# Ten half-size landing tiles for the weights in place of five, and what was moved along with them, in a two-layer hybrid decoder kernel

## The chip, the cores and the metric

The kernel runs on one core of one Trainium2 chip. The metric is the device time of one launch in microseconds (us). Three runs of the kernel before gave 985.4, 985.72 and 986.92 us, a median of 985.72 us. Five engines work side by side and wait for each other by semaphores: TensorE (PE, with its weight load PEld), VectorE (DVE), ScalarE (ACT), GpSimd (POOL) and SyncE (SP). SP computes nothing here: it issues transfers, one after the other, and a transfer that has to wait holds all that stand behind it in SP's list. ACT and POOL issue a few transfers too.

## The reference

Two layers, each with an FFN, a mixer of three attention groups, and a second FFN, over 256 tokens of width 1024, all in float32:

```python
for l in range(DEPTH):                                     # DEPTH = 2
    h = h + 0.5 * swiglu(rms_norm(h, ffn1_norm[l]), ffn1_w_gate[l], ffn1_w_up[l], ffn1_w_down[l])
    h = h + hybrid_mixer(rms_norm(h, mix_norm[l]), w_in[l], ..., w_out[l], cos, sin)
    h = h + 0.5 * swiglu(rms_norm(h, ffn2_norm[l]), ffn2_w_gate[l], ffn2_w_up[l], ffn2_w_down[l])
# swiglu(x, g, u, d) = (silu(x @ g) * (x @ u)) @ d,  the inner width is 2816
```

The mixer projects to 3592 columns, runs a top-64 sparse attention (A, four heads), a block attention (B, four heads) and a forgetting attention with a gate (C, eight heads), and projects back to 1024. All weights, some 190 MB, are read from HBM once.

## The kernel before

**Weights as a stream.** Every product of float32 numbers is made of three matmuls: a number is split into a rounded high part and the rest, and high by high, high by low and low by high are summed in PSUM. So each piece of weights goes through three hands: a transfer brings it into a landing tile (`raw`), ACT makes the high part (`wh`, L278), DVE subtracts to get the low part (`wl`, L282), and PE uses both. The piece in which ACT, DVE and PE work is a *unit*: 128 partitions by 1024 numbers, 512 KB. `Stream` (L75) writes down, before anything runs, the list of all transfers (`raws`) and of all units in the order of use. In the kernel before a transfer brings 128 by 2048 numbers, 1 MB, that is two units, and there are five landing tiles.

**What sets the order.** The engines' instructions stand in the order in which the Python code emits them (`tc.manual_schedule()`). After each unit of PE work `stepped` or the mixer's loop calls `Weights.pump` (L223), which emits the high part of one unit, the low part of the one before it and any addition of weights that has become possible. When the last unit of a landing tile has its low part, `used` (L257) counts the tile as done and `issue` (L198) emits the next transfer on SP. That transfer waits on SP until the tile is free. `W.hold = True` stops such transfers from being emitted, so that others can be put on SP first; `W.free()` lets them go on.

**Exchanges through memory.** To turn a block of activations, DVE transposes 32 by 32 squares (L480), SP writes them to DRAM (`hd`, `xd`, `gd` and `pd`, L481), and four transfers read them back turned (`hT`, `xT`, `spare`, `tab`, L485). Each exchange has two writes, one for each half of the tokens, and the reads wait for both.

**An FFN** runs over chunks c of 512 inner columns: gate, up, then the down products of the chunk before. Chunks 0, 1 and 3 are plain. Chunks 2 and 4 use `seven` (L164 and L629): seven products in place of eight, for which sums of weights (`wide`, L249) and of activations are made. `seven_forms` (L577) makes the activations' sums once for each FFN, in five steps set by `after(1 + 3 * i, fn)` (L632): `differences`, then the forms f1, f2, f3 and f4, each split into high and low (L609, L611, tiles `fva`, `fp`, `fpT`, `fqs`, `fg`). Then come 256 last columns, whose exchange `hd2` has half the size, and `tail` (L809), which does the last down products in quarters q = 0 to 3 (token half q % 2, column half q // 2) and prepares the next stage's normalised input: a residual for each quarter (L496), writes of two column blocks to memory (`send`), reading them back (`fetch`) and splitting them (`rest`, L453 and L454). Block one goes out after q = 0 and 1, block two after q = 2 and 3. A third part is turned on PE (L424). The tail of the second layer's last FFN is `finish`, without a next stage.

Where `n_far` is 4 (a stage that ends before an FFN), `fetch` of block two puts two of the four reads on ACT and two on SP; where it is 2 (before a mixer), all four are on SP.

Of the kernel before, what the change touches and what calls it, by code (L numbers as in the profile page):

```python
# [31 lines left out]

RAW_BUFS = 5
SPLIT_BUFS = 8
# [35 lines left out]
class Stream:  # L70
# [15 lines left out]
    def ffn(self, ffn, l, first=False):  # L86
        gate, up, down = (f"{ffn}_w_{x}" for x in ("gate", "up", "down"))

        def units(r, us=(0, 1)):
            self.units += [(r, 2 * i, 2) for i in us]  # L90

        def chunk(c, hf, kind):
            if c < NC:
                return self.raw(4, 512, [(gate if kind == "g" else up, l, 4 * hf, 512 * c, 512, 0)])
            return self.raw(4, 512, [(gate, l, 4 * hf, 512 * c, 256, 0), (up, l, 4 * hf, 512 * c, 256, 256)])

        def downs(n):
            for _ in range(n):
                i = done[0] % 2
                if not i:  # L100
                    last[:] = [self.raw(2, D, [(down, l, done[0], 0, D, 0)])]
                done[0] += 1
                self.units.append((last[0], i, 1))

        done, last = [0], []
        for c in range(NC):
            if not c:
                for hf in range(2):
                    r = [chunk(c, hf, kind) for kind in "gu"]
                    if first and not hf:  # L110
                        for i in range(2):
                            for x in r:
                                units(x, (i,))
                    else:
                        for x in r:
                            units(x)
# [16 lines left out]
    def seven(self, chunk, c, downs, n_down):  # L133

        def form(r, *add):
            self.units += [(r, 2 * i, 2) + add for i in range(2)]

        r11, r12, r22 = chunk(c, 0, "g"), chunk(c, 0, "u"), chunk(c, 1, "u")
        r21 = chunk(c, 1, "g")
        own = -c - 1  # L140
        form(r11)
# [9 lines left out]
    def mixer(self, l):  # L151
        raws = {}
        for name, us in MIX_START + [(c[0], range(4)) for c in CHUNKS[2:]]:
            cols = dict(CHUNKS)[name]
            n = sum(c[1] for c in cols)
            for u in us:
                hf = u // 2
                if (name, hf) not in raws:
                    raws[name, hf] = self.raw(4, n, [("w_in", l, 4 * hf, c, w, o) for c, w, o in cols])
                self.units.append((raws[name, hf], 2 * (u % 2), 2))  # L160
        for j in range(0, 8, 2):
            r = self.raw(2, D, [("w_out", l, OUT_ORDER[j], 0, D, 0)])
            self.units += [(r, i, 1) for i in range(2)]

# [11 lines left out]
class Weights:  # L176
# [22 lines left out]
    def issue(self, most=2):  # L199
        upto = min(len(self.raws), self.n_raw_done + RAW_BUFS, self.n_dma + most)  # L200
        while not self.hold and self.n_dma < upto:
            a, b, _, _ = self.raws[self.n_dma]
            self.raw_tiles[self.n_dma] = self.raw_pool.tile([P, 2048], F32, name="raw", tag="raw")[:, :a * b]
            if self.n_dma >= self.by_hand:
                self.load(self.n_dma, 0, a)
            self.n_dma += 1
# [4 lines left out]

    def free(self, most=2):
        self.hold = False
# [19 lines left out]
    def part(self, raw, i, shape):  # L233
        if raw < 0:
            return self.home[:, i:i + shape]
        a, b, _, _ = self.raws[raw]
# [64 lines left out]
def kernel(ctx: ExitStack, tc: tile.TileContext, x, xt, weights, small, const, out):  # L301
# [49 lines left out]
    W = Weights(tc, raw_pool, split_pool, weights)  # L351
    W.by_hand = 4
    W.n_raw_done -= RAW_BUFS - 4
    W.issue(RAW_BUFS)
    for k in range(4):
        if k:
            load_xT(k, 1)
        for i in range(2):
            W.load(i, k, k + 1)
    for i in (2, 3):  # L360
        for k in (0, 2):
            if i == 2:
                for m in range(4 + k, 6 + k):
                    load_xT(m, 1)
            W.load(i, k, k + 2)
    W.n_raw_done += RAW_BUFS - 4
    W.issue(RAW_BUFS)

# [131 lines left out]
    def ffn(norm, nxt, aside=None, first=False):  # L500
# [78 lines left out]
        def seven_forms():  # L579
# [256 lines left out]
    def tail(acc, rhs, ks, factor, make_norm, late=None, early=()):  # L836
# [19 lines left out]
        if early:  # L856
# [4 lines left out]
            for q in range(4):  # L861
# [30 lines left out]
        W.pump()  # L892
        nxt.fetch(8 - n_far, n_far, A if n_far > 2 else None)
        W.free()
# [638 lines left out]
```

## Time and profile before

| What | Value |
|---|---|
| runs | 985.4, 985.72, 986.92 us; median 985.72 |
| profiled execution | 985.31 us, its span 983.6 us, TensorE clock 1.00 |
| PE busy | 971.6 us, 99% of the span, 4608 matmuls |
| PEld, DVE, ACT, POOL busy | 81%, 83%, 62%, 17% |
| transfers | 226.64 MB, 230 GB/s on average; SP's queue 59.9% of 16 engines' span |
| weight transfers on SP | 160 of 1024 KB, median 6.8 us from issue to landing, and 20 smaller |

A row of the groups or of the list in order of time reads: line, engine, operation, tile written and tiles read, shapes, count; and in square brackets the idle time of the engine just before it and what ended that. In the chain of waits a row has its start, its length and what the time went to; a DMA row runs from the issue to the landing. "SPq" and "ACTq" are issues of transfers by those engines. A row of stages has the busy time of PE, PEld, DVE, ACT and POOL, the clock, the mean busy share of the 16 DMA engines and the GB/s.

### The profile page before, as it was taken

How to read it: one execution, taken by the hardware profiler on the slowest of the kernel's cores; microseconds unless marked ns; L12 is line 12 of the kernel's file. 1: busy time of each engine (PE TensorE's matmuls, PEld its weight loads, DVE VectorE, ACT ScalarE, POOL GpSimd, SP SyncE). 2: the span in 40 equal slices, each digit the busy share in tenths (PEclk: the TensorE clock that was granted, in tenths of full speed). 3: DMA queues.
4: the chain of work that ended last, by engine and by line, in shares of the span. 5: the costliest groups of instructions: out<-in, count | busy, mean ns of one | idle time of the engine just before them, and what ended most of it. 6: DMA issues, size and time to landing. Idle time of an engine off the chain costs nothing.

```text
span 983.6 us, 13303 instructions
## 1 busy us (share of the span) xinstructions
PE 971.6 (99%) x4608; PEld 800.4 (81%) x4608; DVE 820.9 (83%) x1284; ACT 610.4 (62%) x1024; POOL 164.1 (17%) x190
## 2 busy tenths in 40 slices
PE   9999999999999999999989999999999999999998
PEld 8878878788878888887868888778888788888877
DVE  6999698689987799779669987976899868998794
ACT  6757465567876657546465555746677856575561
POOL 0000002177530000000000000030866200000000
PEclk9999999999999999999999999999999999999999
DMA  9878866684554777766767677766645547687561
GB/s 336 311 211 330 279 220 217 221 305 149 193 190 142 268 226 251 261 194 257 267 254 265 181 261 248 276 204 223 261 172 210 166 133 290 197 293 280 155 262 59
DMA packets 81299, 226.64 MB, mean 230 GB/s; under 512 B 18240, under 2 KB 48208, under 8 KB 60752
## 3 DMA queue, kind: packets, MB, share of 16 engines
q1 hardware_dynamic: 76112, 213.16, 59.9%
q0 software_dynamic: 2304, 8.39, 4.9%
q10 hardware_dynamic: 2816, 4.24, 1.5%
q8 instruction: 36, 0.59, 0.2%
q14 instruction: 31, 0.25, 0.1%
HBM read 208.44 MB, written 17.33 MB: 230 GB/s over the span
## 4 chain that ended last, share of the span: by engine, by line
PE 78%; DVE 8%; DMA 7%; ACT 3%; issue 2%; SPq 2%; ACTq 0%; DVEq 0%
PE ps_gu L389 54%; PE ps_acc L389 22%; DVE wl L282 4%; DMA xd<-tmp 2%; DMA hT<-hd 2%; DMA hd<-tmp 2%; SPq L485 2%; ACT wh L278 1%; DVE tmp L480 1%; ACT hh L571 1%; DMA xT<-xd 1%; PE ps_gu L1314 1%; DVE tmp L559 1%; DVE trunk L496 1%; PE ps_acc L982 1%
## 5 line engine op out<-in xcount | busy, mean ns | idle before, releaser
L389 PE MATMUL ps_gu<-wh,xhl 128*128 128x512 f32 (+2 forms) x1600 | 494.9, 386 | 3.2 <-ACT xhl L453 2.7
L282 DVE TENSOR_TENSOR wl<-raw,wh 128x1024 fp32r<-128x1024 f32 (+2 forms) x340 | 404.3, 1225 | 16.3 <-ACT wh L278 16.2
L278 ACT CAST wh<-raw 128x1024 fp32r<-128x1024 f32 (+2 forms) x340 | 340.8, 1039 | 87.3 <-DMA raw<-in_weights_dram 38.4
L389 PEld LDWEIGHTS ps_gu<-wh,xhl 128*128 128x128 f32 x1600 | 298.6, 188 | 64.8 <-ACT xhl L453 3.5
L389 PE MATMUL ps_gu<-wl,xhl 128*128 128x512 f32 (+2 forms) x800 | 306.2, 384 | 0.1
L389 PEld LDWEIGHTS ps_gu<-wl,xhl 128*128 128x128 f32 x800 | 150.3, 188 | 28.4 <-DVE wl L282 0.5
L389 PE MATMUL ps_acc<-wh,hh 128*128 128x512 f32 (+1 forms) x352 | 136.8, 389 | 0.5 <-ACT hh L571 0.5
L389 PE MATMUL ps_acc<-wh,hl 128*128 128x512 f32 (+1 forms) x352 | 136.5, 388 | 0.0
L389 PE MATMUL ps_acc<-wl,hh 128*128 128x512 f32 (+1 forms) x352 | 136.3, 387 | 0.0
L278 ACT CAST wh<-wide 128x1024 fp32r<-128x1024 f32 x48 | 49.6, 1052 | 76.7 <-DVE wide L249 53.4
L389 PEld LDWEIGHTS ps_acc<-wh,hh 128*128 128x128 f32 x352 | 66.1, 188 | 14.6 <-ACT hh L571 1.4
L389 PEld LDWEIGHTS ps_acc<-wh,hl 128*128 128x128 f32 x352 | 66.1, 188 | 14.2 <-DVE hl L572 0.6
L389 PEld LDWEIGHTS ps_acc<-wl,hh 128*128 128x128 f32 x352 | 66.1, 188 | 13.3
L247 POOL DMA_DIRECT2D raw<-in_weights_dram x16 | 14.3, 893 | 372.1 <-DMA raw<-in_weights_dram 184.6
L571 ACT CAST hh<-hT 128x256 fp32r<-128x256 f32 x88 | 29.4, 403 | 55.5 <-DMA hT<-hd 55.4
L282 DVE TENSOR_TENSOR wl<-wide,wh 128x1024 fp32r<-128x1024 f32 x48 | 57.6, 1214 | 2.9 <-ACT wh L278 2.7
L572 DVE TENSOR_TENSOR hl<-hT,hh 128x256 fp32r<-128x256 f32 x88 | 32.2, 426 | 23.6 <-ACT hh L571 23.6
L559 DVE SCALAR_TENSOR_TENSOR tmp<-ps_gu,y_n,tmp 128x512 f32<-128x512 f32 (+1 forms) x32 | 21.4, 667 | 30.5 <-PE ps_gu L389 24.6
L400 POOL TENSOR_TENSOR y_n<-msq,minus_half 128x2 f32<-128x2 f32 x6 | 7.7, 1288 | 217.5 <-DVE msq L399 137.5
L249 DVE TENSOR_TENSOR wide<-wide,raw 128x1024 f32<-128x1024 f32 x32 | 39.1, 1222 | 0.6
L480 DVE STREAM_TRANSPOSE tmp<-tmp 128x512 f32<-128x512 f32 (+1 forms) x52 | 34.6, 668 | 1.7
L389 PE MATMUL ps_gu<-wh,fp 128*128 128x512 f32 x96 | 33.6, 390 | 0.9 <-ACT tmp L651 0.9
(259 smaller groups left out, 1093.8 us busy)
## 6 DMA issues: line engine op xcount, KB each, us to landing
raw<-in_weights_dram SPq DMA_DIRECT2D x160, 1024.0 KB, 6.8
hd<-tmp SPq DMA_DIRECT2D x40, 256.0 KB, 2.0
hT<-hd SPq DMA_DIRECT2D x80, 128.0 KB, 2.6
raw<-in_weights_dram POOLq DMA_DIRECT2D x16, 512.0 KB, 6.3
raw<-in_weights_dram SPq DMA_DIRECT2D x4, 768.0 KB, 8.3
raw<-in_weights_dram SPq DMA_DIRECT2D x4, 672.0 KB, 7.6
raw<-in_weights_dram SPq DMA_DIRECT2D x8, 256.0 KB, 4.6
raw<-in_weights_dram SPq DMA_DIRECT2D x4, 512.0 KB, 6.9
```

Of the source, the lines that this page charges most:

```text
L247: self.nc.gpsimd.dma_start(self.part(*unit), self.kept(rs[0], *unit[1:]), accum_op=ALU.add)
L249: self.nc.vector.tensor_tensor(self.part(*unit), *(self.part(r, *unit[1:]) for r in rs), op=ALU.add)
L278: self.nc.scalar.copy(hv, src)
L282: (engine or self.nc.vector).tensor_tensor(lv, self.srcs[self.n_low], hv.bitcast(F32), op=ALU.subtract)
L389: T.matmul(o, l, r, start=start, stop=stop, skip_group_check=True)
L480: V.transpose(o.rearrange("p (j b c) -> p b j c", j=4, b=n), x.rearrange("p (b j c) -> p b j c", b=n, j=4))
L485: (other if other and j > 1 else eng).dma_start(to[32 * j:32 * j + 32], sc[:, j].rearrange("(i r) x -> r i x", r=32))
L496: V.scalar_tensor_tensor(d, ps, factor, d, op0=ALU.mult, op1=ALU.add)
L559: V.scalar_tensor_tensor(a, u, norm.r[:, t:t + 1], a, op0=ALU.mult, op1=ALU.mult)
L571: A.copy(by(hh), x)
L572: V.tensor_tensor(by(hl), x, by(hh).bitcast(F32), op=ALU.subtract)
L982: T.transpose(ps[:, i * S + t * P:i * S + (t + 1) * P], xs[t][:, (j + i) * P:(j + i + 1) * P], ident)
```

## The change

**Tiles.** `RAW_BUFS` goes from 5 to 10 and a landing tile from 128 by 2048 to 128 by 1024, so the room stays at 5 MB. Each unit has its own transfer and its own tile. The order of units, of ACT's and DVE's splitting and of PE's work stays; what changes is that a tile is free, and the next transfer emitted, after every unit and not after every second one. The sums in `wide` get two names (`own`), one for each half.

**Hold.** In chunk 4 of each FFN the hold begins after the products of f4 and no longer before them; in chunk 2 it stays. `free` lets four transfers go where it let two.

**Tail.** The pump of quarter 3 moves to the end of quarter 2, ahead of the hold, so one weight transfer is emitted between the two writes of block two. `fetch` puts all four reads on SP.

**Forms.** The steps 1, 4, 7, 10, 13 become 1, 2, 4, 6, 13.

```diff
-RAW_BUFS = 5
+RAW_BUFS = 10
@@ Stream.ffn
+        def piece(c, k, kind):
+            if c < NC:
+                return self.raw(2, 512, [(gate if kind == "g" else up, l, k, 512 * c, 512, 0)])
+            return self.raw(2, 512, [(gate, l, k, 512 * c, 256, 0), (up, l, k, 512 * c, 256, 256)])
 
         def chunk(c, hf, kind):
-            if c < NC:
-                return self.raw(4, 512, [(gate if kind == "g" else up, l, 4 * hf, 512 * c, 512, 0)])
-            return self.raw(4, 512, [(gate, l, 4 * hf, 512 * c, 256, 0), (up, l, 4 * hf, 512 * c, 256, 256)])
+            return [piece(c, 4 * hf + k, kind) for k in (0, 2)]
...
-                i = done[0] % 2
-                if not i:
-                    last[:] = [self.raw(2, D, [(down, l, done[0], 0, D, 0)])]
+                self.units.append((self.raw(1, D, [(down, l, done[0], 0, D, 0)]), 0, 1))
                 done[0] += 1
-                self.units.append((last[0], i, 1))
@@ Stream.seven
-        own = -c - 1
+        own = [-2 * c - 1, -2 * c - 2]
@@ Weights
-            self.raw_tiles[self.n_dma] = self.raw_pool.tile([P, 2048], F32, name="raw", tag="raw")[:, :a * b]
+            self.raw_tiles[self.n_dma] = self.raw_pool.tile([P, 1024], F32, name="raw", tag="raw")[:, :a * b]
...
-    def free(self, most=2):
+    def free(self, most=4):
@@ seven_forms
-            for i, fn in enumerate((differences, f1, f2, lambda: split("f3", two, 3), lambda: split("f4", one, 1))):
-                after(1 + 3 * i, fn)
+            for i, fn in zip((1, 2, 4, 6, 13), (differences, f1, f2, lambda: split("f3", two, 3), lambda: split("f4", one, 1))):
+                after(i, fn)
@@ seven
-            W.hold = True
-            form(y, "f4", False, True)
+            W.hold = c < NC - 1
+            form(y, "f4", False, True)
+            W.hold = True
...
-            W.free(1 if last else 2)
+            W.free(2 if last else 4)
@@ tail, the quarters
                 if q == 3:
                     W.hold = True
-                    W.pump()
                     nxt.rest()
                 residual(q, acc[q], factor)
...
+                if q == 2:
+                    W.pump()
             W.pump()
-            nxt.fetch(8 - n_far, n_far, A if n_far > 2 else None)
+            nxt.fetch(8 - n_far, n_far)
             W.free()
```

PE's and POOL's instructions stand in the same order as before, and DVE's differ only around the forms. Three places show what moved.

SP at the end of the first FFN of layer 0, from the reading back of chunk 3's exchange to the next stage's block one. Before (`hd` is chunk 4's exchange, `hd_1510` the last 256 columns', `gb` a small table, `xd_1637` block one):

```order
L485 DMA hT<-hd 32x8x128 x4
L220 DMA raw<-in_weights_dram 128x2048 x6
L481 DMA hd<-tmp 128x512 x2
L485 DMA hT<-hd 32x8x128 x4
L220 DMA raw<-in_weights_dram 128x2048
L348 DMA gb<-in_heads_dram 128x384
L481 DMA hd_1510<-tmp 128x256 x2
L485 DMA hT<-hd_1510 32x8x64 x4
L220 DMA raw<-in_weights_dram 128x2048
L220 DMA raw<-in_weights_dram 128x1344 x2
L220 DMA raw<-in_weights_dram 128x2048
L481 DMA xd_1637<-tmp 128x256 x2
```

With the change (`hd_1576` and `xd_1711` are the same exchanges):

```order
L479 DMA hT<-hd 32x8x128 x4
L214 DMA raw<-in_weights_dram 128x1024 x14
L475 DMA hd<-tmp 128x512 x2
L479 DMA hT<-hd 32x8x128 x4
L214 DMA raw<-in_weights_dram 128x1024
L343 DMA gb<-in_heads_dram 128x384
L475 DMA hd_1576<-tmp 128x256 x2
L479 DMA hT<-hd_1576 32x8x64 x4
L214 DMA raw<-in_weights_dram 128x672
L214 DMA raw<-in_weights_dram 128x1024
L214 DMA raw<-in_weights_dram 128x672 x3
L214 DMA raw<-in_weights_dram 128x1024 x3
```

Ahead of chunk 4's exchange there were six transfers of 1 MB and are 14 of 512 KB, 1 MB more; ahead of the last columns' exchange there was 1 MB and is half of that; ahead of block one the bytes are the same.

ACT at the end of the second FFN of layer 0, from the splitting of block one to that of block two. Before:

```order
L453 ACTIVATE xhl<-xT,gx 128x256 x2
L458 ACTIVATE tmp,ss_4639<-trunk 128x512
L278 CAST wh<-raw 128x1024
L485 DMA xT<-xd_4734 32x8x128 x2
L278 CAST wh<-raw 128x1024 x4
L453 ACTIVATE xhl<-xT,gx 128x256 x4
```

With the change:

```order
L447 ACTIVATE xhl<-xT,gx 128x256 x2
L452 ACTIVATE tmp,ss_4817<-trunk 128x512
L273 CAST wh<-raw 128x1024 x5
L447 ACTIVATE xhl<-xT,gx 128x256 x4
L273 CAST wh<-raw 128x1024 x2
```

ACT's two reads, and with them its wait for the writes of block two, are gone from between the casts.

DVE around the forms in the first FFN of layer 0 (`fva` belongs to f1, `fp` to f2, `fpT` to f3, `hl` is the low part of chunk 0's hidden activations). Before:

```order
L282 TENSOR_TENSOR wl<-raw,wh 128x1024 x3
L572 TENSOR_TENSOR hl<-hT,hh 128x256 x4
L282 TENSOR_TENSOR wl<-raw,wh 128x1024
L611 SCALAR_TENSOR_TENSOR fva_395<-tmp,fva_394 128x512
L597 TENSOR_TENSOR tmp<-tmp,xhl 128x512 x2
L282 TENSOR_TENSOR wl<-raw,wh 128x1024 x3
L611 SCALAR_TENSOR_TENSOR fp<-tmp,fp 128x128 x4
```

With the change:

```order
L277 TENSOR_TENSOR wl<-raw,wh 128x1024 x2
L605 SCALAR_TENSOR_TENSOR fva_415<-tmp,fva_414 128x512
L591 TENSOR_TENSOR tmp<-tmp,xhl 128x512 x2
L277 TENSOR_TENSOR wl<-raw,wh 128x1024
L566 TENSOR_TENSOR hl<-hT,hh 128x256 x4
L277 TENSOR_TENSOR wl<-raw,wh 128x1024
L605 SCALAR_TENSOR_TENSOR fp<-tmp,fp 128x128 x4
```

The low part of f1 and the two sums for f2 now stand ahead of `hl`, and f2's and f3's low parts come two to four units' low parts sooner. From the first `wl<-wide` on, DVE's order is what it was.

More of the change, by code (lines that the diff above doesn't have):

```diff
@@ L87, in ffn, with units @@
         gate, up, down = (f"{ffn}_w_{x}" for x in ("gate", "up", "down"))
-        def units(r, us=(0, 1)):
-            self.units += [(r, 2 * i, 2) for i in us]
+        def units(rs):
+            self.units += [(r, 0, 2) for r in rs]
+        def piece(c, k, kind):
+            if c < NC:
+                return self.raw(2, 512, [(gate if kind == "g" else up, l, k, 512 * c, 512, 0)])
+            return self.raw(2, 512, [(gate, l, k, 512 * c, 256, 0), (up, l, k, 512 * c, 256, 256)])
         def chunk(c, hf, kind):
-            if c < NC:
-                return self.raw(4, 512, [(gate if kind == "g" else up, l, 4 * hf, 512 * c, 512, 0)])
-            return self.raw(4, 512, [(gate, l, 4 * hf, 512 * c, 256, 0), (up, l, 4 * hf, 512 * c, 256, 256)])
+            return [piece(c, 4 * hf + k, kind) for k in (0, 2)]
         def downs(n):
             for _ in range(n):
-                i = done[0] % 2
-                if not i:
-                    last[:] = [self.raw(2, D, [(down, l, done[0], 0, D, 0)])]
+                self.units.append((self.raw(1, D, [(down, l, done[0], 0, D, 0)]), 0, 1))
                 done[0] += 1
-                self.units.append((last[0], i, 1))
-        done, last = [0], []
+        done = [0]
         for c in range(NC):
@@ L108, in ffn @@
                 for hf in range(2):
-                    r = [chunk(c, hf, kind) for kind in "gu"]
                     if first and not hf:
-                        for i in range(2):
-                            for x in r:
-                                units(x, (i,))
-                    else:
-                        for x in r:
-                            units(x)
+                        for k in (0, 2):
+                            units([piece(c, k, kind) for kind in "gu"])
+                    else:
+                        for kind in "gu":
+                            units(chunk(c, hf, kind))
                 continue
@@ L135, in form @@
         def form(r, *add):
-            self.units += [(r, 2 * i, 2) + add for i in range(2)]
+            for i in range(2):
+                self.units.append((r[i], 0, 2, *(x[i] for x in add[:-1]), *add[-1:]))
         r11, r12, r22 = chunk(c, 0, "g"), chunk(c, 0, "u"), chunk(c, 1, "u")
         r21 = chunk(c, 1, "g")
-        own = -c - 1
+        own = [-2 * c - 1, -2 * c - 2]
         form(r11)
@@ L151, in mixer @@
     def mixer(self, l):
-        raws = {}
         for name, us in MIX_START + [(c[0], range(4)) for c in CHUNKS[2:]]:
@@ L156, in mixer @@
             for u in us:
[L157 to L163, printed above, removed]
+                self.units.append((self.raw(2, n, [("w_in", l, 2 * u, c, w, o) for c, w, o in cols]), 0, 2))
+        for j in range(8):
+            self.units.append((self.raw(1, D, [("w_out", l, OUT_ORDER[j], 0, D, 0)]), 0, 1))
     def packed(self, inputs):
@@ L234, in part @@
         if raw < 0:
+            i = 2 * ((-raw - 1) % 2)
             return self.home[:, i:i + shape]
@@ L351 @@
     W = Weights(tc, raw_pool, split_pool, weights)
-    W.by_hand = 4
-    W.n_raw_done -= RAW_BUFS - 4
+    W.by_hand = 8
+    W.n_raw_done -= RAW_BUFS - 8
     W.issue(RAW_BUFS)
@@ L358 @@
         for i in range(2):
[L359 to L366, printed above, removed]
+            W.load(2 * (k // 2) + i, k % 2, k % 2 + 1)
+    for i in range(4):
+        if i < 2:
+            for m in range(4 + 2 * i, 6 + 2 * i):
+                load_xT(m, 1)
+        W.load(4 + i, 0, 2)
+    W.n_raw_done += RAW_BUFS - 8
     W.issue(RAW_BUFS)
@@ L892, in tail @@
         W.pump()
-        nxt.fetch(8 - n_far, n_far, A if n_far > 2 else None)
+        nxt.fetch(8 - n_far, n_far)
         W.free()
```

## The prediction

> **What bounds the kernel now.** I read the page first, for the whole.
>
> ```profile
> span 983.6 us, 13303 instructions
> PE 971.6 (99%) x4608; PEld 800.4 (81%) x4608; DVE 820.9 (83%) x1284; ACT 610.4 (62%) x1024; POOL 164.1 (17%) x190
> ```
>
> PE is busy for 971.6 of 983.6 us, and no matmul is added or taken away. So the change can only act on the stretches in which PE stands still. These come from PE's list in order of time. I kept two ordinary rows and those after the pauses that the change may reach.
>
> ```profile
> 44.80 0.39 PE L389 MATMUL ps_acc<-wl,hh 128*128 128x512 f32 x1
> 45.02 0.39 PE L389 MATMUL ps_acc<-wh,hl 128*128 128x512 f32 x1
> ...
> 187.25 0.44 PE L424 MATMUL ps_acc<-ident,trunk 128*128 128x128 f32 x2 [1.18 <-DVE trunk L496]
> 480.32 0.50 PE L389 MATMUL ps_acc<-wh,hh 128*128 128x512 f32 x1 [0.35 <-ACT hh L571]
> 496.67 0.50 PE L389 MATMUL ps_gu<-wh,xhl 128*128 128x512 f32 x1 [1.98 <-ACT xhl L453]
> 506.23 0.50 PE L389 MATMUL ps_gu<-wh,xhl 128*128 128x512 f32 x1 [0.68 <-ACT xhl L453]
> 507.17 0.73 PE L389 MATMUL ps_gu<-wh,xhl 128*128 128x512 f32 x2 [0.21 <-DVE xhl L454]
> 660.27 0.50 PE L389 MATMUL ps_acc<-wh,hh 128*128 128x512 f32 x1 [0.19 <-ACT hh L571]
> 676.47 0.44 PE L424 MATMUL ps_acc<-ident,trunk 128*128 128x128 f32 x2 [1.26 <-DVE trunk L496]
> ```
>
> Full-width matmuls start 0.22 us apart but are drawn 0.39 long, and the first after a pause is drawn 0.50. So a pause costs its idle time plus about 0.27 us (0.17 and 0.11). They lie at three transitions: first FFN to mixer in layer 0 (1.18, which with 0.17 is about 1.3 us), second FFN of layer 0 to first FFN of layer 1 (0.35, 1.98, 0.68 and 0.21, each plus 0.27, make 0.6, 2.25, 0.95 and 0.5), and first FFN to mixer in layer 1 (0.19 and 1.26: 0.45 and 1.4). Together 7.5 us. What is late there stands in the chain of waits.
>
> ```profile
> 162.49 4.48 DMA hd<-tmp
> ...
> 172.23 1.26 DVE wl L282
> 175.72 5.62 DMA xd<-tmp
> ...
> 470.96 4.22 DMA hd<-tmp
> 484.56 7.57 DMA xd<-tmp
> 498.91 1.98 DMA xd<-tmp
> ```
>
> A write to memory that meets empty queues lands in 1.98 us. The write of block one takes 5.62 us in layer 0's first transition and 7.57 us in the second. SP's list tells why.
>
> ```profile
> 159.92 0.40 SPq L220 DMA_DIRECT2D raw<-in_weights_dram  x1
> 167.15 1.80 SPq L485 DMA_DIRECT2D hT<-hd  x4
> 169.00 2.05 SPq L220 DMA_DIRECT2D raw<-in_weights_dram  x4
> 174.60 1.45 SPq L481 DMA_DIRECT2D xd<-tmp  x2
> ```
>
> Four weight transfers (3.5 MB here, 4 MB in the second transition) are issued the moment the reading of the last columns' exchange has left SP, and block one queues behind their bytes. So block one lands when that exchange was read, plus the time of those bytes; and the exchange itself waited behind the 1 MB issued at 159.92.
>
> **The change part by part.** *Half the bytes ahead of the last columns' exchange.* The next rows are of the stage view; the last two columns are the DMA engines' busy share and GB/s.
>
> ```profile
> 12.00:18.00 6.00, 6.00 (x28) 4.96 (x27) 5.04 (x11) 5.38 (x13) 0.00 (x0) 1.00 1.00 351
> 133.00:138.00 5.00, 5.00 (x24) 4.12 (x22) 5.00 (x8) 5.00 (x9) 0.00 (x0) 1.00 0.45 184
> 138.00:153.00 15.00, 14.84 (x64) 11.67 (x63) 14.97 (x16) 9.41 (x11) 0.00 (x0) 1.00 0.93 347
> 161.50:164.50 3.00, 3.00 (x15) 2.49 (x14) 2.77 (x7) 2.28 (x6) 0.00 (x0) 1.00 1.00 314
> 171.00:179.00 8.00, 8.00 (x39) 6.66 (x38) 4.43 (x7) 2.88 (x7) 4.18 (x9) 1.00 1.00 394
> 480.00:489.00 9.00, 8.68 (x40) 7.14 (x41) 4.32 (x8) 3.81 (x9) 0.00 (x0) 1.00 1.00 411
> ```
>
> At 314 GB/s the 1 MB takes 3.3 us; half of it is 1.7 us less. The most that can be won is down to an unhindered write: 4.48 - 1.98 = 2.5 us in the first transition, 4.22 - 1.98 = 2.2 in the second. The least is nothing, if the 1 MB more ahead of chunk 4's exchange passes the delay on. I take 1.8, near the 1.7, because 133 to 138 us shows the queues 45% busy just before the backlog of 138 to 153: tiles freed by halves put transfers there sooner, and that pays for the extra 1 MB.
>
> *The same bytes in smaller transfers ahead of block one.* From the rows, the opening (12 to 18 us), where weights come as 512 KB and less, moved 351 GB/s with the engines fully busy; the bursts of 1 MB transfers moved 394 and 411. That is 0 to 15% of a burst of 8 to 10 us: 0 to 1.5 us lost. I take 0.5, since the opening also has smaller pieces in it. So block one is read 1.8 - 0.5 = 1.3 us sooner at each of the three transitions.
>
> On SP eight issues replace four: at 0.51 each (2.05 for four) 4.1 us from 169.00, so 173.1, and block one is ready only at 174.60; with the exchange 1.8 us sooner the cover is 3.3 us. The eighth waits for the low part that ends at 173.5 (the chain's 172.23 plus 1.26), still 1.1 us ahead. If an issue took over 0.9 us, block one would be late by the rest.
>
> [...]
>
> *What the transitions give back.* First: PE waits 1.3, the gain is 1.3. Third: the waits are 0.45 + 1.4 on one chain, the gain 1.3. Second: 0.6 + 2.25 on one chain, the gain 1.3, and then block two, where ACT's list has this:
>
> ```profile
> 501.87 3.89 ACT L278 CAST wh<-raw 128x1024 fp32r<-128x1024 f32 x4 [2.04 <-DMA xd<-tmp]
> 505.67 1.70 ACT L453 ACTIVATE xhl<-xT,gx 128x256 fp32r<-128x256 f32 x4
> ...
> 465.96 0.32 SPq L485
> 470.08 0.72 ACT hh L571 x2
> ```
>
> *The reads on SP alone.* ACT stood 2.04 us behind its own two reads, and its four casts then ran into the splitting of block two, for which PE waits at 506.23 and 507.17. Without the reads the casts end at 503.7. Four reads of this size on SP alone took 4.1 us from the first issue to ACT's first use (465.96 to 470.08); put at 500.97, where the second block's reads were issued (498.91 + 1.98, and the issue), that is 505.1, so the splitting starts 0.6 us sooner, and DVE's, no longer behind its low parts, right after. The waits of 0.95 and 0.5 shrink to about 0.35 together: 1.1 us won. Bounds: 0.6 if only the start moves, 1.45 if both waits go. At the two places ahead of a second FFN the list has no wait of PE of this kind; costed at nothing, the cover being ACT's same four casts of 3.9 us.
>
> *The transfer between the two writes of block two* has 498.91 - 492 = 7 us of empty queue for 1.3 to 1.7 us: nothing. *Holding later in chunk 4* is the 1 MB above.
>
> *The forms.* They move 0.69 + 1.42 us of DVE work ahead of chunk 0's `hl`, in a stage in which DVE is full.
>
> ```profile
> 38.50:61.00 22.50, 22.50 (x101) 18.65 (x100) 22.36 (x32) 13.57 (x24) 1.92 (x2) 1.00 0.92 305
> 41.97 1.43 DVE L572 TENSOR_TENSOR hl<-hT,hh 128x256 fp32r<-128x256 f32 x4
> 44.45 0.69 DVE L611 SCALAR_TENSOR_TENSOR fva<-tmp,fva 128x512 fp32r<-128x512 f32 x1
> 45.17 1.42 DVE L597 TENSOR_TENSOR tmp<-tmp,xhl 128x512 f32<-128x512 f32 x2
> 67.54 1.05 ACT L278 CAST wh<-wide 128x1024 fp32r<-128x1024 f32 x1 [3.57 <-DVE wide L249]
> 70.07 0.50 PE L389 MATMUL ps_gu<-wh,fp 128*128 128x512 f32 x1 [0.85 <-ACT tmp L651]
> ```
>
> `hl` starts at 44.1 and its first quarter is there at 44.5; PE reads it at 45.02, so the cover is 0.5 us, and each us beyond costs one. The wait at 70.07 (1.1 us with its restart) is that of ACT's copy L651 behind a cast that waits for DVE's sum L249. DVE is busy 22.36 of 22.5 us up to there with the same work in sum, so I leave this wait: 0, with 1.1 won as the other bound.
>
> The sum: 1.3 + 1.3 + 1.1 + 1.3 = 5.0 us. The profiled execution took 985.31 (span 983.6), which gives 980.3; the median of the runs is 0.4 higher, so 980.3 to 980.7, and I say 980.4.
>
> **The rivals.** *More*: the exchange gains its 2.2, the smaller transfers lose nothing and the forms free the wait at 70.07: 1.3 + 2.2 + 1.4 + 1.85 + 1.1 = 7.9, so 977.5. For it, the empty stretch 133 to 138; against it, the full DVE. *The bytes only change places*: the 1 MB sent ahead of chunk 4's exchange delays it, its reads and the half transfer behind them, and block one is read when it was; only ACT's 1.1 stays: 984.4. For it, the backlog of 138 to 153 at 93%; against it, the same empty stretch. *Slower*: half-size transfers move at a lower rate. Place: the bursts of 3.5 to 4 MB ahead of block one. The point is where the burst grows by more than the 1.8 won, 8.5 us times 21%. [...] For it, these rows of the issues (KB each, us to landing): a half as slow as a whole.
>
> ```profile
> raw<-in_weights_dram SPq DMA_DIRECT2D x160, 1024.0 KB, 6.8
> raw<-in_weights_dram SPq DMA_DIRECT2D x4, 512.0 KB, 6.9
> ```
>
> Against it, those four halves queued behind others in the opening, where 351 GB/s still moved, 15% below at most.
>
> **How the numbers follow.** The forecast (4 to 6.5 us won) has 0.60, more 0.15, bytes in other places 0.14, slower 0.11. A measurement of this kernel tells about 0.2%, 2 us, from no change. The first two cases are faster: 0.75, and 0.01 of the third; the third else is no change: 0.13; the last is slower: 0.11. The range leaves out most of the slower case and the tail of the best one: 977.4 to 985.0; the likeliest case's own is 978.8 to 981.6.
>
> **What would show it.** In the profile after: the last columns' `hd` in the chain near 2.5 to 3 us in place of 4.48 and 4.22; PE's rows near 187 and 676 without idle time, those near 480 and 497 at 1 us together; no ACT row with 2.04 behind `xd`; the wait for L651 still there. SP's burst of eight must be issued by the time block one is ready. Wrong it would be if block one's write lasts as long as before (5.6 to 7.6 us) counted from an exchange that is no sooner, or if the stage of the burst shows under 330 GB/s.

## The result and the profile after

The changed kernel takes 980.06 us (median of four runs, 979.35 to 980.88), against 985.76 us for the kernel before on the same chip (four runs, 985.4 to 986.92). The ratio is 0.9942, with a 95% interval of 0.9925 to 0.996, so it is 0.4 to 0.75% faster. In a second comparison (`after_again` below, six runs against eleven of the kernel before) it was 0.9947, interval 0.993 to 0.9963. The forecast was 980.4 us.

The page after, first two lines:

```profile
span 978.3 us, 13761 instructions
PE 970.5 (99%) x4608; PEld 801.0 (82%) x4608; DVE 822.3 (84%) x1284; ACT 611.2 (62%) x1024; POOL 167.2 (17%) x190
```

PE's list in order of time, the rows after a pause that answer to those shown before (L383 was L389, L418 was L424, L447 was L453, L645 was L651):

```profile
69.52 0.50 PE L383 MATMUL ps_gu<-wh,fp 128*128 128x512 f32 x1 [0.84 <-ACT tmp L645]
185.78 0.44 PE L418 MATMUL ps_acc<-ident,trunk 128*128 128x128 f32 x2 [0.26 <-DVE trunk L490]
493.33 0.50 PE L383 MATMUL ps_gu<-wh,xhl 128*128 128x512 f32 x1 [0.74 <-ACT xhl L447]
502.48 0.50 PE L383 MATMUL ps_gu<-wh,xhl 128*128 128x512 f32 x1 [0.23 <-ACT xhl L447]
670.91 0.44 PE L418 MATMUL ps_acc<-ident,trunk 128*128 128x128 f32 x2 [0.70 <-DVE trunk L490]
```

The wait at 70 us is as long as it was (0.85 before). Those of 1.18, 1.98, 0.68 and 1.26 us are 0.26, 0.74, 0.23 and 0.70. Those of 0.35 (480.32), 0.21 (507.17) and 0.19 (660.27) have no row any more.

PE runs the same 4608 matmuls in the same order, so the start of each can be set against its start before. The difference grows to 5.2 us in these steps: 0.53 in the opening (up to 7 us), 0.92 in the first transition, 2.74 in the second (0.64 at `hh`, 1.23 for block one, 0.87 for block two), 1.39 in the third (0.80 and 0.59), and 0.27 back in layer 1's mixer. All the rest is the same to 0.1 us.

Where the transitions' time went shows in SP's list at the second one, before and after. A row is one group of issues: start, time from the first to the end of the last, and how many; the last columns' exchange is `hd` and `hT`, block one `xd`.

```profile
468.35 2.93 SPq L481 DMA_DIRECT2D hd<-tmp  x2
475.26 2.64 SPq L485 DMA_DIRECT2D hT<-hd  x4
477.95 2.19 SPq L220 DMA_DIRECT2D raw<-in_weights_dram  x4
483.30 1.59 SPq L481 DMA_DIRECT2D xd<-tmp  x2
```

```profile
466.94 2.59 SPq L475 DMA_DIRECT2D hd<-tmp  x2
472.18 1.80 SPq L479 DMA_DIRECT2D hT<-hd  x4
474.03 5.85 SPq L214 DMA_DIRECT2D raw<-in_weights_dram  x8
481.09 1.69 SPq L475 DMA_DIRECT2D xd<-tmp  x2
```

Before, the second write was issued by 468.35 + 2.93 = 471.28 and could be read at 475.26, 4.0 us later; after, it takes from 469.53 to 472.18, 2.65 us. From that read to the landing of block one it was 475.26 to 492.13 (the chain's 484.56 + 7.57), 16.9 us. After, the chain of waits has these rows (495.57 is block two, the others block one):

```profile
175.18 4.86 DMA xd<-tmp
482.46 6.53 DMA xd<-tmp
495.57 1.96 DMA xd<-tmp
659.88 5.27 DMA xd<-tmp
```

So it is 472.18 to 488.99, 16.8 us. The exchange is read sooner, and from there block one takes as long behind halves (transfers of 512 KB) as behind wholes (1 MB).

### The profile page after: what moved, and what is told of

It is laid out like the page before. It is cut to its first block, busy times and chain, and to the rows that moved or that the text cites. A ratio compares the mean times of both kernels' runs of the same rounds, so it can differ in the third digit from the quotient of the medians.

```text
span 978.3 us, 13761 instructions
## 1 busy us (share of the span) xinstructions
PE 970.5 (99%) x4608; PEld 801.0 (82%) x4608; DVE 822.3 (84%) x1284; ACT 611.2 (62%) x1024; POOL 167.2 (17%) x190
## 4 chain that ended last, share of the span: by engine, by line
PE 86%; DVE 5%; DMA 5%; ACT 3%; issue 1%; SPq 1%; ACTq 0%; POOL 0%; DVEq 0%; POOLq 0%
PE ps_gu L383 58%; PE ps_acc L383 25%; DMA xd<-tmp 2%; DVE wl L277 2%; ACT wh L273 2%; DMA hT<-hd 1%; DMA xT<-xd 1%; SPq L479 1%; DVE tmp L474 1%; DMA hd<-tmp 1%; PE ps_gu L1310 1%; PE ps_acc L978 1%; DVE trunk L490 1%; ACT hh L565 0%; DVE tmp L553 0%
## 5 line engine op out<-in xcount | busy, mean ns | idle before, releaser
L383 PE MATMUL ps_gu<-wh,xhl 128*128 128x512 f32 (+2 forms) x1600 | 494.6, 386 | 1.1 <-ACT xhl L447 1.0
L383 PEld LDWEIGHTS ps_gu<-wh,xhl 128*128 128x128 f32 x1600 | 298.6, 188 | 62.0 <-DVE tmp L665 1.9
L383 PE MATMUL ps_gu<-wl,xhl 128*128 128x512 f32 (+2 forms) x800 | 306.2, 384 | 0.1
L383 PEld LDWEIGHTS ps_gu<-wl,xhl 128*128 128x128 f32 x800 | 150.3, 188 | 28.5 <-DVE wl L277 0.5
L383 PE MATMUL ps_acc<-wh,hh 128*128 128x512 f32 (+1 forms) x352 | 136.6, 388 | 0.0
L383 PE MATMUL ps_acc<-wh,hl 128*128 128x512 f32 (+1 forms) x352 | 136.3, 387 | 0.0
L383 PE MATMUL ps_acc<-wl,hh 128*128 128x512 f32 (+1 forms) x352 | 136.3, 387 | 0.0
L383 PEld LDWEIGHTS ps_acc<-wh,hl 128*128 128x128 f32 x352 | 66.1, 188 | 13.5
L383 PEld LDWEIGHTS ps_acc<-wh,hh 128*128 128x128 f32 x352 | 66.1, 188 | 13.5
L383 PEld LDWEIGHTS ps_acc<-wl,hh 128*128 128x128 f32 x352 | 66.1, 188 | 13.4
L383 PE MATMUL ps_gu<-wh,fp 128*128 128x512 f32 x96 | 33.6, 390 | 0.8 <-ACT tmp L645 0.8
```

Source lines behind the costliest of these rows:

```text
L383: T.matmul(o, l, r, start=start, stop=stop, skip_group_check=True)
```

## The experiments

Each of the four sets has its own runs of the kernel before on the same chip; their medians were 985.13, 985.01, 985.47 and 983.63 us. Ratios are against these. The changed kernel itself ran again only in the second set (`after_again`); in the other sets a run is compared with it by the ratios. T1, T2 and T3 are the transitions at 187, 480 to 507 and 660 to 676 us.

### First set: which part of the change it is

**`tiles_only`**: the ten tiles alone.

```diff
-for i, fn in zip((1, 2, 4, 6, 13), ...)
+for i, fn in zip((1, 4, 7, 10, 13), ...)
-            W.hold = c < NC - 1
-            form(y, "f4", False, True)
-            W.hold = True
+            W.hold = True
+            form(y, "f4", False, True)
# the tail's W.pump() back into q == 3, fetch with A if n_far > 2
```

> Ten tiles of half the size alone; hold, forms' steps, the place of the tail's pump and ACT's two reads as in the kernel before. SP's list then has 1 MB ahead of the last columns' exchange as before, and half a transfer more (0.5 MB) ahead of block one. My theory, by which the bytes ahead of the two exchanges decide: block one is no sooner, up to 1.3 us later at each transition, and ACT's 1.1 us is not won: 985 to 988 us. The rival, by which tiles that come free one by one are the gain: some 982 us.

Measured: 990.08 us, ratio 1.0054 (1.0037 to 1.0071). Alone, the tiles make the kernel slower, by more than I expected. SP and PE at T2:

```profile
470.37 2.19 SPq L475 DMA_DIRECT2D hd<-tmp  x2
477.61 1.80 SPq L479 DMA_DIRECT2D hT<-hd  x4
479.45 5.03 SPq L214 DMA_DIRECT2D raw<-in_weights_dram  x9
498.81 0.50 PE L383 MATMUL ps_gu<-wh,xhl 128*128 128x512 f32 x1 [2.85 <-ACT xhl L447]
```

Two halves ahead of the exchange are the old 1 MB, which now takes 5.05 us from write to read; nine halves ahead of block one are 0.5 MB more than the four wholes. PE's waits at the three transitions are 2.6, 2.85 and 2.5 us.

**`hold_back`**: the changed kernel with only chunk 4's hold back ahead of f4.

```diff
-            W.hold = c < NC - 1
-            form(y, "f4", False, True)
-            W.hold = True
+            W.hold = True
+            form(y, "f4", False, True)
```

> The changed kernel with chunk 4's hold ahead of f4 again. SP's list has 1 MB ahead of the last columns' exchange and half a transfer more ahead of block one than the changed kernel. My theory: the exchange is read 1.7 us later and block one 1.3 to 2 us later at each of three transitions, so 3.9 to 6 us lost: 983.5 to 986 us, ACT's 1.1 us kept. If the hold is worth nothing: 980.1 us.

Measured: 989.86 us, ratio 1.005 (1.0031 to 1.0069). Without the later hold nothing of the gain is left. The same view:

```profile
469.18 2.20 SPq L475 DMA_DIRECT2D hd<-tmp  x2
475.30 2.43 SPq L479 DMA_DIRECT2D hT<-hd  x4
477.78 4.80 SPq L214 DMA_DIRECT2D raw<-in_weights_dram  x9
677.14 0.50 PE L418 MATMUL ps_acc<-ident,trunk 128*128 128x128 f32 x2 [3.23 <-DVE trunk L490]
```

From write to read it is 3.9 us again, as in the kernel before. The loss of some 10 us against the change is larger than the 3.9 to 6 expected; the profiled execution loses 7.5 us, of which about 1.7 are a stretch at half clock after the pause of 3.23 us, an estimate (last section).

**`moves_only`**: the kernel before, five tiles of 1 MB, with the moves alone.

```diff
-for i, fn in enumerate(...): after(1 + 3 * i, fn)
+for i, fn in zip((1, 2, 4, 6, 13), ...): after(i, fn)
+            W.hold = c < NC - 1
             form(y, "f4", False, True)
+            W.hold = True
# the tail's W.pump() after q == 2, fetch with all reads on SP
```

> The kernel before with its five tiles of 1 MB, and only the moves: the later hold, four reads on SP, the tail's pump, the forms' steps. SP's list then has 7 MB ahead of chunk 4's exchange, nothing ahead of the last columns' exchange, and 3.31 or 4 MB ahead of block one as before. My theory (bytes): the last columns' write lands in 2.0 us, so block one is up to 2.2 us sooner at each transition, and ACT's 1.1 us is won: 978.5 to 981 us, no worse than with ten tiles. The rival, by which only ten tiles let the empty stretch ahead of chunk 4's backlog be used: the seventh 1 MB delays chunk 4's exchange by its 2.6 us and all behind it: 984 to 987 us.

Measured: 982.9 us, ratio 0.9974 (0.9964 to 0.9984): less than half of the gain, between what the theory and the rival expected. The exchange of the last columns is as early at T2 as with ten tiles, but block two pays. Chain and PE at T2:

```profile
496.35 3.92 DMA xd<-tmp
505.00 0.50 PE L389 MATMUL ps_gu<-wh,xhl 128*128 128x512 f32 x1 [2.01 <-ACT xhl L453]
```

The whole megabyte that now stands between block two's two writes makes the second write 3.92 us long, where before and after the change it took 1.98 and 1.96, and PE waits 2.0 us.

**`burst3`**: the changed kernel, with three of the eight transfers ahead of block one and five behind its reads.

```diff
         split = back(4 * NC, 2, sc)
-        W.free()
+        W.free(3)
+        W.hold = nxt is not None
...
                 if q == 1:
                     nxt.fetch(2, 2)
+                    W.free(8)
```

> The changed kernel with only the first three weight transfers let go behind the last columns' reads (1.2 or 1.5 MB in place of 3.3 or 4), and the other five behind block one's reads. My theory: block one's write lands in 2 to 3 us in place of 4.9 to 6.5, PE's waits of 0.4, 0.9 and 0.9 us at the three transitions go, and the five are early enough, since their units are used 10 us later: 977.5 to 979 us. The rival: five transfers 6 to 8 us later run into block two's exchange and leave ACT without weights: 981 to 985 us.

Measured: 983.36 us, ratio 0.9985 (0.9975 to 0.9994), so most of the gain is lost again. Both halves of the expectation came true at once. PE has no wait for block one at any transition. But the five transfers stand ahead of block two (2.5 MB, and the tail's half), whose second write took 5.83 us at T2, and PE waited 2.40 us for it:

```profile
493.36 5.83 DMA xd<-tmp
503.99 0.50 PE L383 MATMUL ps_gu<-wh,xhl 128*128 128x512 f32 x1 [2.40 <-ACT xhl L447]
```

### Second set: what is left when the worst of it is taken out

**`after_again`**: the changed kernel itself.

> The changed kernel itself once more, beside the others of this set and in more runs. My theory: the same 0.994 of the time before, since its waits at the three transitions are of a fixed size. The rival, that the first comparison of four runs was lucky: nearer to 0.997.

Measured: 979.87 us, 0.9947 (0.993 to 0.9963). The first result holds.

**`moves_no_pump`**: `moves_only` with the tail's pump where it was, so that no megabyte goes between block two's writes.

```diff
                 if q == 3:
                     W.hold = True
+                    W.pump()
                     nxt.rest()
...
-                if q == 2:
-                    W.pump()
```

> Five tiles of 1 MB with the later hold, four reads on SP and the forms' steps, but the tail's pump in its old place, so no 1 MB goes between block two's two writes. With that 1 MB the second write took 3.9 us in place of 2.0 and PE waited 1.3 us longer for block two. My theory: this wait goes, 980 to 981.5 us, nearly the whole gain without smaller tiles. The rival: the 1 MB transfers' late reading of chunk 4's exchange (1.3 to 1.9 us late) costs the rest, and the time stays at 983 us.

Measured: 981.12 us, 0.9957 (0.9941 to 0.9974). The second write takes 1.98 us again and PE waits as briefly as after the change:

```profile
496.19 1.98 DMA xd<-tmp
503.03 0.50 PE L389 MATMUL ps_gu<-wh,xhl 128*128 128x512 f32 x1 [0.21 <-ACT xhl L453]
```

So 3.9 of the 5.1 us that `after_again` gained in this set come without a smaller tile. The other 1.25 us is less than the intervals can tell.

**`fetch_back`**: two of block two's four reads on ACT again.

```diff
-nxt.fetch(8 - n_far, n_far)
+nxt.fetch(8 - n_far, n_far, A if n_far > 2 else None)
```

> The changed kernel with two of block two's four reads on ACT again ahead of an FFN. My theory: ACT stands 2 us behind its reads at the second transition and its casts run into the splitting of block two: 0.8 to 1.1 us lost, 981 us, 0.995 of the time before. The rival, by which the two reads come sooner on a second queue and ACT's casts have room: no loss, 980.1 us.

Measured: 980.46 us, 0.9951 (0.9934 to 0.9969), 0.6 us above `after_again`, on the expected side but within the interval. The rows show the mechanism. ACT's list first in `fetch_back`, then in the changed kernel:

```profile
496.33 0.85 ACTq L479 DMA_DIRECT2D xT<-xd  x2
497.23 3.90 ACT L273 CAST wh<-raw 128x1024 fp32r<-128x1024 f32 x4 [1.99 <-issue]
501.03 1.70 ACT L447 ACTIVATE xhl<-xT,gx 128x256 fp32r<-128x256 f32 x4
```

```profile
495.46 4.83 ACT L273 CAST wh<-raw 128x1024 fp32r<-128x1024 f32 x5
501.92 1.71 ACT L447 ACTIVATE xhl<-xT,gx 128x256 fp32r<-128x256 f32 x4 [1.63 <-DMA xT<-xd]
```

With its reads on ACT, ACT loses 1.99 us and its casts run up to the splitting; without, ACT is done 1.63 us before block two is there. PE's waits for block two in `fetch_back` are back at nearly the old size (0.68 and 0.21 before):

```profile
501.58 0.50 PE L383 MATMUL ps_gu<-wh,xhl 128*128 128x512 f32 x1 [0.61 <-ACT xhl L447]
502.52 0.74 PE L383 MATMUL ps_gu<-wh,xhl 128*128 128x512 f32 x2 [0.20 <-DVE xhl L448]
```

`fetch_back` gained more for block one here, so the waits alone don't settle it; but counted from the issue of block two's second write (494.31 here), PE goes on after 7.3 to 7.4 us and waits a second time 0.9 us later in the three traces with two reads on ACT (`before`, `tiles_only`, `fetch_back`), and goes on after 6.8 to 6.9 us with no second wait in five with all on SP (`after`, `after_again`, `forms_back`, `pump_back`, `moves_no_pump`).

**`hold_at2`**: five transfers ahead of block one, three behind its reads.

```diff
         W.free()
         stepped()
         stepped()
+        W.hold = nxt is not None
...
                     nxt.fetch(2, 2)
+                    W.free(8)
```

> The changed kernel with five weight transfers (1.8 or 2.5 MB) let go behind the last columns' reads and three behind block one's reads; before it was three and five. The seven us between the last columns' reads and block one's write hold five transfers. My theory: block one's write meets empty queues as with three (2 us), the waits of 0.4, 0.9 and 0.9 us go, and the three that are left are through before block two's second write: 977.5 to 979 us, 0.992 of the time before. The rival, that any transfer put behind block one's reads delays block two as the five did (1.3 to 2.1 us each): 981 us or more.

Measured: 979.54 us, 0.9944 (0.9925 to 0.9962), the same as the changed kernel and not the 977.5 to 979 us of the theory. The profiled execution is the slowest of the six (982.74 us). In it the rival was right on block two at T2: with three halves and the tail's one ahead of it the second write took 5.33 us, and PE's wait for block one turned into one for block two.

```profile
493.33 5.33 DMA xd<-tmp
503.47 0.50 PE L383 MATMUL ps_gu<-wh,xhl 128*128 128x512 f32 x1 [2.00 <-ACT xhl L447]
```

### Third set: the two edits that were costed at nothing, and a better order

**`forms_back`**: the forms' steps 1, 4, 7, 10, 13 in the changed kernel.

```diff
-for i, fn in zip((1, 2, 4, 6, 13), ...)
+for i, fn in zip((1, 4, 7, 10, 13), ...)
```

> The changed kernel with the forms' steps 1, 4, 7, 10, 13 as before. My theory: no difference that can be told (DVE is full from 26 to 72 us and does the same work in sum; the wait of 1.0 us at 70 us stays): 980 us. The rivals: the early forms won something in the first FFN, then 981 us or more; or they cost some of it, then 979 us or less.

Measured: 979.99 us, 0.9944 (0.993 to 0.9958). No difference that can be told from the changed kernel's 0.9942 and 0.9947.

**`pump_back`**: the tail's pump in quarter 3 again in the changed kernel.

```diff
                     W.hold = True
+                    W.pump()
                     nxt.rest()
...
-                if q == 2:
-                    W.pump()
```

> The changed kernel with the tail's pump in the last quarter again, so no transfer goes between block two's two writes. My theory: half a transfer there meets 4 us of empty queue and costs nothing, as block two's second write took 1.96 us both before and after: 980 us. The rival, from the whole 1 MB at this place that cost 1.9 us of that write: 979 us or less.

Measured: 980.6 us, 0.9951 (0.9934 to 0.9969). No difference that can be told. Block two's second write takes 2.00 us at T2 without the half ahead of it and 1.96 with it. So half a transfer at this place costs nothing that shows; the whole one of `moves_only` did.

**`late3_tab`**: the changed kernel, with five transfers ahead of block one and then none until block two's reads are issued; and none between the mixer's `gd` and `pd` exchanges.

```diff
         W.free()
         stepped()
         stepped()
+        W.hold = nxt is not None
...
 def blocks(tiles, n, name, to):
     ...
     from_memory(sc, to, nc.sync)
+    W.hold = name == "gd"
```

> The changed kernel with five weight transfers let go behind the last columns' reads, none between block one and the end of block two's exchange (three more and the tail's one wait until block two's reads are issued), and none between the two exchanges of the mixer's last group. With three behind block one's reads, block two's second write had taken 5.0 us in place of 2.0 at the second transition. My theory: PE's waits for block one (0.4, 0.9, 0.9 us in the changed kernel) go, block two is as early as block one lets it be, and the 0.3 to 0.9 us wait for the mixer's table in layer 1 goes: 976.5 to 978 us, 0.992 of the time before. The units of the late transfers have 6 to 10 us of margin. The rival: four to five us of empty queues at each of three places are missing later, weights come late in the chunks behind and the time is 980 us or more.

Measured: 976.74 us (976.65 to 977.33), 0.9913 (0.9898 to 0.9927): faster than both kernels, by some 3 us more than the change. SP at T2, the waits of PE and the page:

```profile
473.40 3.19 SPq L214 DMA_DIRECT2D raw<-in_weights_dram  x5
480.64 1.69 SPq L475 DMA_DIRECT2D xd<-tmp  x2
484.65 1.80 SPq L479 DMA_DIRECT2D xT<-xd  x4
488.44 3.96 SPq L475 DMA_DIRECT2D xd<-tmp  x2
494.20 1.80 SPq L479 DMA_DIRECT2D xT<-xd  x4
496.04 5.60 SPq L214 DMA_DIRECT2D raw<-in_weights_dram  x9
```

```profile
span 974.9 us, 13763 instructions
PE ps_gu L383 <- ACT tmp L645: 1.7, 2, 0.9
PE ps_gu L383 <- POOL minus_half L336: 1.0, 1, 1.0
```

Block one is read 2.3 us after its second write is issued (480.64 + 1.69 to 484.65), block two 1.8 us after. Of the nine halves in the last row four had been held back: in the changed kernel three of them go out ahead of block one and one between block two's writes, and five behind its reads. At T2 none of their units makes PE wait in the next stage. What the hold between `gd` and `pd` gave of the 3 us was not measured apart. Of PE's waits only those of the opening and of ACT's copy L645 are long enough for the list. One of the latter, at 620.84 us, has grown from 0.10 to 0.86, since ACT waited there for a reading back of `hT`; whether the new order causes that was not tried.

### Fourth set: the same order with whole tiles

**`late_whole`**: `moves_no_pump` (five tiles of 1 MB) with the hold of `late3_tab`.

```diff
         W.free()
         stepped()
         stepped()
+        W.hold = nxt is not None
```

> Five tiles of 1 MB with the moves (later hold, four reads on SP, forms' steps, the pump in its old place), and the order of the fastest version: three wholes (2.3 or 3 MB) behind the last columns' reads, and none until block two's reads are issued. My theory: what is sent ahead of which exchange decides and not the size of a transfer, so PE's waits for block one (0.1, 1.2 and 1.0 us with whole tiles and without this order) go: 978 to 979.5 us, 0.993 of the time before. The rival: with whole tiles chunk 4's exchange is read 1.5 to 2 us later than with halves and the last columns' with it; then block one is no sooner, 981 us and 0.996 as without this order.

Measured: 977.86 us (977.17 to 978.3), 0.9944 (0.993 to 0.9958) of a kernel before that took 983.63 us on this chip. PE's waits for blocks one and two are gone here too. Against `late3_tab`, in the profiled executions, its PE ends 1.6 us later: it loses 0.96 us in the opening, which varies by as much between `after` and `forms_back`, and 1.1 us where the low part of a unit is late, since chunk 4's exchange ran later, and then wins 0.4 us back. The second of these shows as:

```profile
169.88 0.50 PE L389 MATMUL ps_acc<-wl,hh 128*128 128x512 f32 x1 [0.43 <-DVE wl L282]
```

So the order of what is sent brings the larger part of the gain with whole tiles too. What the halves add is left open: the two kernels ran on different chips, the medians are 1.1 us apart, but against the kernel before on its own chip `late3_tab` won 8.7 us and `late_whole` 5.8. `late_whole` also lacks the hold between `gd` and `pd`. In the one comparison on the same chip (`moves_no_pump` with `after_again`) the halves and the pump together made 1.25 us, less than can be told.

### The two intervals, over all profiled executions

One execution's burst varies by a microsecond or two, so the terms are better read from several. A is from the start of the issue of the last columns' second write to its first read, B from there to the first read of block one, in us, from SP's issues in each trace. (The 4.0 and 2.65 us above count from the end of that issue, some 0.3 us later.) The changed kernel's order up to block one is that of `after`, `after_again`, `fetch_back`, `forms_back` and `pump_back`.

| Kernel (executions) | ahead of A, of B at T2 | A: T1, T2, T3 | B: T1, T2, T3 |
|---|---|---|---|
| before (1) | 1 MB, 4 MB | 4.67, 4.30, 4.63 | 14.34, 17.31, 15.48 |
| `moves_only`, `moves_no_pump` (2) | none, 4 MB | 2.76, 3.10, 3.56 | 14.38, 17.50, 15.48 |
| the change (5) | 0.5 MB, 4 MB in halves | 3.02, 2.60, 2.75 | 14.70, 17.47, 15.78 |
| `hold_back` (1) | 1 MB in halves, 4.5 MB | 4.51, 4.25, 4.38 | 15.30, 17.35, 17.17 |
| `tiles_only` (1) | 1 MB in halves, 4.5 MB | 4.58, 5.38, 5.14 | 16.01, 17.11, 16.39 |
| `late3_tab` (1) | 0.5 MB, 2.5 MB in halves | 3.57, 2.80, 3.21 | 11.78, 13.09, 11.84 |

In the five executions of the change B at T2 goes from 16.24 to 18.27. B is not the burst alone: with 2.5 MB in `late3_tab`, where block one is read 1.5 to 2.3 us after its second write is issued, 11.8 to 13.1 us are left. A is not shorter with nothing ahead than with 0.5 MB, probably because with whole tiles chunk 4's exchange, which comes ahead of it, is itself read late (466.14 and 466.61 us at T2, 464.27 to 465.19 in the change).

PE's starts against those of the kernel before tell the same by place, in us gained, with one execution of the kernel before as the measure of all five:

| Execution | opening | T1 | T2: `hh`, block one, block two | T3 | layer 1's mixer |
|---|---|---|---|---|---|
| `after` | 0.53 | 0.92 | 0.64, 1.23, 0.87 | 1.39 | -0.27 |
| `after_again` | 0.26 | 1.40 | 0.64, 0.87, 0.82 | 1.92 | -0.84 |
| `fetch_back` | 0.35 | 1.40 | 0.64, 2.21, 0.02 | 1.02 | -0.89 |
| `forms_back` | -0.55 | 1.30 | 0.64, 0.82, 0.93 | 2.02 | -0.04 |
| `pump_back` | 0.50 | 0.63 | 0.64, 0.71, 0.92 | 1.78 | 0.00 |

## Why the prediction was right, and where its working was wrong

**Half the bytes ahead of the last columns' exchange: 1.8 forecast, 1.65, 1.7 and 1.9 measured** (the change against before in column A). The size is right. The source is not as I put it. I took it for the work of the smaller tiles and counted the later hold as its price ("holding later in chunk 4 is the 1 MB above"). It is the other way round. `hold_back` and `tiles_only` show 1 MB still ahead of the exchange, in two halves, and A about as long as before (4.3 to 5.4 us); and whole tiles with the later hold have the short A. What is sent before chunk 4's exchange, in a stretch where the queues had room (45% busy from 133 to 138 us before, 95% in `after`), need not be sent before the last columns' one. My lower bound for this part ("the least is nothing") was also wrong for the tiles alone: they add 0.5 MB ahead of block one, and cost 5 us, in six runs with a mean clock of 0.994 to 0.999 (last section).

**Smaller transfers: 0.5 us lost forecast, 0.0 to 0.3 measured**, column B of the change against the three executions with whole tiles (14.37, 17.4 and 15.48). The rival that was to end on the slower side, for which the burst had to grow by more than 1.8 us, is refuted: within this spread block one is read as soon after the exchange with eight pieces of 3.5 to 4 MB ahead of it as with four. The rate did fall: in the first 10 us of the burst at T2 the DMA engines moved 298 GB/s in `after` (474.03 to 484.03 us) and 359 before (477.95 to 487.95), at T1 332 (167.04 to 177.04) and 344 (169 to 179). So the prediction's sign of being wrong, under 330 GB/s in the stage of the burst, came at T2 by this stretch (not from 480 to 489 us, with 359), but block one was not read later for it.

**What the transitions gave back: 1.3 + 1.3 + 1.3 forecast, 0.92 + 1.87 + 1.39 in the profiled execution, 1.1 + 1.8 + 1.6 in the mean of the five.** At T2 the 1.87 is the 0.64 at `hh` and 1.23 for block one. The chain there moved by more than 1.3, since the 0.5 us that the smaller transfers were to cost did not come and the last columns' second write was itself issued 0.3 us sooner, counted from PE's place. At T1 and T3 PE still waits 0.26 and 0.70 us, where the prediction looked for no idle time.

**The reads on SP: 1.1 forecast, 0.82 to 0.93 in the four executions with them and 0.02 in `fetch_back`, 0.6 between the medians** of `fetch_back` and `after_again`. The mechanism is as told (ACT's 1.99 us), only the size was a little high: from SP's first read to ACT's splitting it took 4.3 us (497.58 to 501.92) and not 4.1, and PE still waits 0.23 us for block two.

**At nothing: the forms, the transfer between block two's writes.** Both right (`forms_back`, `pump_back`). But "7 us of empty queue for 1.3 to 1.7 us" held only because the transfer is half a tile: a whole one there cost block two's second write 1.9 us, and PE waited 1.3 us longer than before the change. This is a place where the smaller tiles pay.

**The wait at 70 us: 0 forecast, 0 measured.**

**What the sum left out.** A term of 0.27 us in layer 1's mixer: one half now goes between the exchanges `gd` and `pd`, and the second one waits behind it. After the change, and in `late3_tab`, where it is held back:

```profile
778.34 0.38 SPq L214 DMA_DIRECT2D raw<-in_weights_dram  x1
779.37 1.24 SPq L475 DMA_DIRECT2D pd<-tmp  x2
784.11 1.80 SPq L479 DMA_DIRECT2D tab<-pd  x4
```

```profile
776.28 1.26 SPq L475 DMA_DIRECT2D pd<-tmp  x2
779.10 1.80 SPq L479 DMA_DIRECT2D tab<-pd  x4
```

From the last write's issue to the read it is 3.5 us in the one and 1.6 in the other. Other executions with the same order there lost up to 0.9 us. And 0.5 us of the profiled gain is the opening. In `after_again` and `forms_back` PE is 0.3 and 1.1 us later there than in `after`, though the first weights land as early (4.08 and 4.11 us, 4.15 in `after`), so this gain is not counted as the change's. The total, 5.0 forecast against 5.2 in the trace and 5.7 and 5.1 between the medians, is closer than its terms: in the profiled execution T1 and the reads gave 0.6 us less than forecast, T2 and T3 as much more, and the mixer and the opening nearly cancel. That much of the hit is luck; the path (exchange, burst, block one) and the wait of ACT are not.

**The rivals.** "More" (977.5) fell short in the change but not in its order: `late3_tab` reached 976.7 by taking part of the burst itself off block one, which the prediction had not thought of. "The bytes only change places" is refuted by column A, "slower" by column B.

## What to carry to other kernels

Small exchanges through memory that share a queue with a stream of weights wait here for what stands ahead of them: at T2 a write took 2.0 us with nothing close ahead (`pump_back`), 3.9 behind 1 MB (`moves_only`), 5.3 behind 2 MB (`hold_at2`) and 5.8 behind 3 MB (`burst3`). (Whether a write put on another engine's queue would pass the stream was not tried.) Count, for each exchange, the megabytes sent ahead of it, and move them to the nearest stretch that ends no exchange: here five 512 KB transfers fit before block one and none between block one and block two, and that order gave 8.7 us in all where tiles of half the size alone lost 5. Smaller tiles alone were no gain here; they let such an order be set in finer steps, and their freed room must then be held back on purpose, or it is filled ahead of the next exchange: without the later hold (`hold_back`) 1 MB stood there again, and the time was 989.86 us.

## What the runs showed of the hardware

**In three traces TensorE ran at half clock for 3.4 us, soon after a pause of 2.0 to 3.2 us.** In `hold_at2` PE waited 2.00 us up to 503.47 and then ran at half clock; `moves_only` (2.01 us up to 505.00) and `hold_back` (3.23 us up to 677.14) show the same. The stage view of `hold_at2`, the clock being the number after POOL's busy time:

```profile
503.00:505.00 2.00, 1.53 (x6) 1.16 (x7) 1.55 (x4) 2.00 (x5) 0.00 (x0) 0.99 0.98 301
505.00:508.00 3.00, 3.00 (x8) 2.34 (x7) 3.00 (x4) 3.00 (x5) 0.00 (x0) 0.50 1.03 418
```

Eight matmuls in 3 us in place of 13 (an estimate from the row of 480 to 489 us before: 40 in 9 us at clock 1.00). The next microsecond has 0.81. `moves_only` has 0.61, 0.50, 0.50 and 0.69 in the four microseconds from 506, `hold_back` 0.69, 0.50, 0.50 and 0.60 in those from 677. In each of the three traces this adds up to 3.4 us at 0.50, so each cost a busy PE half of that, some 1.7 us, an estimate, beside the pause. By the same rows the clock fell 0.2 us (`hold_back`), 1.2 us (`moves_only`) and 1.5 us (`hold_at2`) after PE had started again. It did not follow every pause: `tiles_only` had three of 2.5 to 2.85 us, with 1.00 in every row of its stage view, and `burst3` one of 2.40, with a mean clock of 1.0 and matmuls 0.23 us apart behind it. What tells the pauses with it from those without was not shown.

The three profiled executions with such a stretch have a mean clock of 0.998. The kernel before, whose longest pause in its profiled execution was 1.98 us, had 0.998 or less in 25 of the 55 runs of the four sets, `hold_back` in seven of seven, `late3_tab` and `late_whole` in none of ten. Whether pauses lowered it in the runs without a trace was not shown. The profiled executions of `before`, `after`, `tiles_only` and `late3_tab` have no such stretch before the last microseconds (mean clocks 1.0, 1.0, 0.999 and 1.0), so the 5.2 and 8.7 us won there are not clock, and `tiles_only` loses 3.6 us there (spans 987.2 and 983.6) without it. How much of the differences between the medians is clock was not measured apart.
